# Map 1's shift in the differential attention: one reduce over adjacent columns instead of a minimum of two operands

## The chip, the cores and the metric

The kernel runs on one core of a Trainium2 chip. The metric is the time of one execution on the device in microseconds (us), less is better. The core's engines run side by side, each through its own list of instructions in order, and wait for each other by semaphores: TensorE (PE) multiplies matrices into PSUM, VectorE (DVE), ScalarE (ACT) and GpSimd (POOL) work on tiles of 128 partitions, and DMA queues, most of them fed by SyncE (SP), move data between the on-chip SBUF and the main memory.

## What is computed

The reference is a block of two layers on 2048 latent tokens and 256 context tokens of width 1024. In each layer one projection feeds four mixers side by side; their outputs are gated, projected and added to the stream. The change is in the first mixer, differential attention, of four heads with two attention maps each:

```python
def attend(qs, ks, vs):
    s = jnp.einsum('mbhqd,mbhkd->mbhqk', qs, ks).astype(F32) * scale
    p = jax.nn.softmax(s, axis=-1)
    w = (p[0] - lam * p[1]).astype(vs.dtype)
    return jnp.einsum('bhqk,bhkv->bhqv', w, vs)
...
o = lax.map(lambda qq: attend(qq, keys, vals), qb)
```

The latent tokens' queries see all 2304 keys. In the first layer there are also queries of the context tokens, which see the 256 context keys alone. The other three mixers are a gated linear recurrence, a windowed attention and an mLSTM.

## The kernel before

Each layer runs in three stages: first projections, then the loop of the differential attention, then the windowed attention, the two recurrences and the output projection. The rest of the layer's projections (`other_blocks`) are not given a stage of their own: they are the **filler** of the attention loop. `pump` issues filler matmuls until a given amount of TensorE work has been handed out, and is called with `FSTEP` between the two score products of a map and with `FGAP` after each map.

The loop goes over units of one head and 128 queries: 72 in layer 0 (of which 8 are context units) and 64 in layer 1. A unit does its map 1 first, then its map 0. `diff_scores(u, m)` (L1036 on) forms the scores of map `m` in two pieces of 1024 and 1280 keys, each in a PSUM buffer `scr` of its own that exists once. Behind each piece a `tensor_reduce` on DVE (L1048) takes the minimum over the keys into a column of the small tile `sm` (128 x 16): columns 2 and 3 for map 1, columns 0 and 1 for map 0. (The exponential is taken with a scale of -1, so the minimum plays the part of the maximum.) Then the minimum of the two columns becomes `u["nm"]`, the shift of the exponential: column 5 for map 1 (L1054), column 4 for map 0 (L1056, with a constant `shf` added). `diff_exp` (L1058 on) has ACT take the exponentials of both pieces out of PSUM with this shift, into tiles `p`, and their sums. Only then may PE write the next map's scores into the two buffers.

`diff_mix(u1, j)` works on the unit before, one piece at a call: for piece 0 three small instructions on `sm` (L1073 to L1075), and then for each piece one big DVE instruction that forms the weights from the two `p` tiles (L1082, by the helper `stt`, L111), a copy to 16 bits on ACT (L1084), the remainder as a subtraction on POOL (L1085, by the helper `tt`, L108), and a transposing DMA into `wt` (L1087). `tc.issue_after(u["nm"].ins)` puts the DVE instructions of `diff_mix` behind the new unit's `nm`. `diff_out` multiplies `wt` with the values of the unit before that one.

PE's order is the program's (`manual_schedule` for PE). The order of DVE, ACT, POOL and SP is made by a planner from planned durations, within the dependencies. In the profile, instructions of the helpers carry the helper's line: the minimum of L1054 stands as `L108 DVE TENSOR_TENSOR sm<-sm`, and the big DVE instruction as `L111 ... p<-p,sm,p`.

Of the kernel before, what the change touches and what calls it, by code (L numbers as in the profile page):

```python
# [15 lines left out]
ALU = mybir.AluOpType  # L16
# [13 lines left out]
AX = mybir.AxisListType  # L30
# [43 lines left out]
def kernel(  # L74
# [8 lines left out]
    V, A, G, PE, SP = nc.vector, nc.scalar, nc.gpsimd, nc.tensor, nc.sync  # L83
# [9 lines left out]
    def mm(o, lhsT, rhs, start, stop):  # L93
        PE.matmul(o, lhsT=lhsT, rhs=rhs, start=start, stop=stop)  # L94
        n = 1
        for d_ in rhs.shape[1:]:
            n *= d_
        pe_ns[0] += max(128, n * 4 if rhs.dtype == F32 else n) / 2.4
# [8 lines left out]
    def tt(e, o, a, b, op):  # L107
        return e.tensor_tensor(out=o, in0=a, in1=b, op=op)  # L108
# [150 lines left out]
    for l in range(n_layers):  # L259
# [768 lines left out]
        with ExitStack() as st2:  # L1028
# [4 lines left out]
            def halves_of(u):  # L1033
                return [(2048, 256)] if u["ctx"] else HALF

            def diff_scores(u, m):  # L1036


                sm, hs = u["sm"], halves_of(u)
                pss = u["s", m] = []  # L1040
                for j, (k0, n) in enumerate(hs):
                    ps = sps.tile([P, 1536 if j else 1024], F32, tag=f"sc{j}", name="scr")
                    for o in range(0, n, 512):
                        w = min(512, n - o)
                        mm(ps[:, o:o + w], u["Qs"][:, m, u["qo"]:u["qo"] + P], u["Ks"][m][:, k0 + o:k0 + o + w], True, True)
                    if j < len(hs) - 1:
                        pump(FSTEP * u["work"])
                    V.tensor_reduce(sm[:, m * 2 + j:m * 2 + j + 1], ps[:, :n], AX.X, ALU.min)  # L1048
                    pss.append(ps)
                o = m * 2  # L1050
                o2 = o + len(hs) - 1

                if m:
                    u["nm"] = tt(V, sm[:, 5:6], sm[:, o:o + 1], sm[:, o2:o2 + 1], ALU.min)  # L1054
                else:
                    u["nm"] = V.tensor_scalar(sm[:, 4:5], sm[:, o:o + 1], sm[:, o2:o2 + 1], shf, ALU.min, ALU.add)  # L1056

# [99 lines left out]
            def pump(ns):  # L1157
                owed[0] += ns
                while owed[0] > 0:
                    t0 = pe_ns[0]  # L1160
                    if next(filler, pump) is pump:
                        owed[0] = 0.0
                        break
                    owed[0] -= pe_ns[0] - t0
# [4 lines left out]
            with tc.manual_schedule(engines=MANUAL):  # L1169
                while True:  # L1170
                    u = next(it, None)
                    if u is None and u1 is None and u2 is None and u3 is None:
                        break
                    if u:
                        diff_scores(u, 1)
                    if u3:
                        diff_out(u3, 1)
                    pump(FGAP * (u["work"] if u else 1.0))
                    if u1:
                        with tc.issue_after(u["nm"].ins) if u else ExitStack():  # L1180
                            diff_mix(u1, 0)
                    if u:
                        diff_exp(u, 1)
                    if u3:
                        diff_norm(u3, 0)
                    if u:
                        diff_scores(u, 0)
                    if u3:
                        diff_norm(u3, 1)
                    if u2:  # L1190
                        diff_out(u2, 0)
                    pump(FGAP * (u["work"] if u else 1.0))
                    if u1:
                        with tc.issue_after(u["nm"].ins) if u else ExitStack():
                            diff_mix(u1, 1)
                    if u:
                        diff_exp(u, 0)
                    u1, u2, u3 = u, u1, u2
# [535 lines left out]
```

## Time and profile before

| | |
|---|---|
| median of 3 runs | 4100.06 us (4084.22 to 4102.09) |
| the profiled execution | 4102.18 us, span 4100.4 us |
| differential attention, layer 0 | 238 to 1260 us |
| differential attention, layer 1 | 2330 to 3285 us |
| busy over the span | PE 3358.2, DVE 2831.4, POOL 2375.0, ACT 2330.9 us |

Times in the trace are counted from the first instruction. A row of a timeline gives the start, the duration, engine, line, operation, the tile written and the tiles read (`out<-in`), the shapes, the count of instructions that are merged in the row, and in brackets the idle time of the engine before it with what ended it.

### The profile page before, as it was taken

Reading aid. Unit: us, or ns where it says so; the run is one execution under the profiler, and the core shown is the slowest. Engines: PE = TensorE matmul, PEld = TensorE weight load, DVE = VectorE, ACT = ScalarE, POOL = GpSimd, SP = SyncE. Lnnn points to the kernel's source line nnn. Section 1 sums busy time; section 2 is a strip of 40 time slices with the busy share of each in tenths; the row PEclk is TensorE's granted clock in tenths of the full one; section 3 lists DMA queues with packets and bytes.
Section 4 is the critical chain, followed back from the end, with each engine's and each line's share of the span. In section 5 each row is a group of like instructions: output and inputs, shape, how many; then the busy total and the mean of one; then the engine's idle time right before and its main releaser. Section 6 shows DMA issues by size and latency. Waiting matters only on the chain. (4 is left out here: it accounts for less than half of the span.)

```text
span 4100.4 us, 77666 instructions
## 1 busy us (share of the span) xinstructions
PE 3358.2 (82%) x29798; PEld 2269.8 (55%) x29798; DVE 2831.4 (69%) x4343; ACT 2330.9 (57%) x4662; POOL 2375.0 (58%) x1701
## 2 busy tenths in 40 slices
PE   6988878888768996888888988778887698758888
PEld 4656645444546765555557466444445476545554
DVE  5158888888896647465544398988888865467665
ACT  4245655556655636566654266656666665456764
POOL 4443455443445538798966535665334564488885
PEclk8999989999989995898889999999998899869999
DMA  6356866667656628577845457667676584366783
GB/s 211 91 149 150 186 136 159 140 141 154 145 128 157 161 95 200 149 194 185 205 119 177 126 125 151 135 140 155 148 162 142 125 193 116 106 162 170 183 194 104
DMA packets 1267259, 622.12 MB, mean 152 GB/s; under 512 B 931972, under 2 KB 1214152, under 8 KB 1266888
## 3 DMA queue, kind: packets, MB, share of 16 engines
q1 hardware_dynamic: 1164520, 490.65, 53.1%
q10 hardware_dynamic: 102368, 126.52, 9.2%
q8 instruction: 234, 3.83, 0.4%
q14 instruction: 137, 1.12, 0.1%
HBM read 291.76 MB, written 131.23 MB: 103 GB/s over the span
## 5 line engine op out<-in xcount | busy, mean ns | idle before, releaser
L108 POOL TENSOR_TENSOR p<-p,p 128x1024 f16<-128x1024 f32 (+2 forms) x264 | 629.4, 2385 | 792.7 <-ACT p L1084 722.8
L105 ACT ACTIVATE p<-scr,sm 128x1024 f32<-128x1024 f32 (+2 forms) x528 | 628.3, 1194 | 417.8 <-DVE sm L1073 145.2
L94 PE MATMUL ptm<-wb,hh 128*128 128x256 f16 (+2 forms) x5024 | 835.6, 273 | 32.6 <-DVE dSs L111 7.9
L1048 DVE TENSOR_REDUCE sm<-scr 128x1 f32<-128x1024 f32 (+2 forms) x528 | 699.3, 1327 | 218.3 <-PE scr L94 214.5
L94 PE MATMUL pfm<-hh,wb 128*128 128x512 f16 (+1 forms) x2592 | 805.7, 375 | 32.7 <-DVE gz L111 10.1
L94 PE MATMUL ptm<-wb,hl 128*128 128x256 f16 (+2 forms) x2512 | 672.1, 273 | 1.7 <-POOL hl L108 1.7
L94 PEld LDWEIGHTS <-wb 128*128 128x128 f16 x3888 | 378.1, 101 | 414.3 <-issue 84.0
L94 PE MATMUL scr<-Ks,Qs 128*128 128x512 f16 (+1 forms) x1296 | 364.8, 381 | 284.5 <-ACT p L105 279.4
L94 PEld LDWEIGHTS <-hh 128*128 128x128 f16 x5024 | 480.1, 100 | 133.9 <-issue 40.0
L94 PE MATMUL pfm<-hl,wb 128*128 128x512 f16 (+1 forms) x1296 | 485.6, 375 | 0.0
L111 DVE SCALAR_TENSOR_TENSOR p<-p,sm,p 128x1024 f32<-128x1024 f32 (+2 forms) x264 | 413.8, 1568 | 8.1
L94 PEld LDWEIGHTS <-Qs 128*128 128x128 f16 x1296 | 130.7, 102 | 425.2 <-issue 354.5
L94 PE MATMUL fx<-wo,mh 128*128 128x512 f16 x1088 | 342.4, 396 | 16.8 <-DVE xt L111 8.5
L1084 ACT CAST p<-p 128x1024 f16<-128x1024 f32 (+2 forms) x264 | 297.7, 1128 | 39.2 <-DVE p L111 33.8
L94 PEld LDWEIGHTS <-wt 128*128 128x128 f16 x4640 | 243.9, 102 | 71.4 <-DMA wt<-p 24.4
L94 PE MATMUL pv<-Vs,wt 128*128 128x128 f16 (+1 forms) x4640 | 258.5, 213 | 21.9 <-DMA wt<-p 13.5
L94 PEld LDWEIGHTS <-hl 128*128 128x128 f16 x2512 | 250.8, 100 | 35.4 <-POOL hl L108 3.4
L108 POOL TENSOR_TENSOR ph<-swp,ph 128x640 f16<-128x640 f32 (+2 forms) x136 | 196.0, 1442 | 53.7 <-ACT ph L1335 44.3
L108 POOL TENSOR_TENSOR E<-lk,cm 128x512 f32<-128x512 f32 (+1 forms) x136 | 204.8, 1506 | 34.6 <-DMA cm<-dhc 17.8
L94 PE MATMUL fx<-wo,mlo 128*128 128x512 f16 x544 | 212.9, 391 | 1.4 <-DVE mlo L108 1.1
L105 ACT ACTIVATE E<-E 128x1024 f32<-128x1024 f32 x136 | 143.2, 1054 | 102.8 <-POOL E L108 98.9
L108 DVE TENSOR_TENSOR QQ<-hq,E 128x512 f32<-128x512 f32 x119 | 143.8, 1214 | 65.2 <-ACT E L105 46.7
(301 smaller groups left out, 6577.2 us busy)
## 6 DMA issues: line engine op xcount, KB each, us to landing
wraw<-in_w_in_dram SPq DMA_DIRECT2D x60, 512.0 KB
dgt<-ga ACTq DMA_DIRECT2D x68, 256.0 KB
r1b<-dr SPq DMA_DIRECT2D x68, 256.0 KB
gtt<-dgt SPq DMA_DIRECT2D x34, 512.0 KB
mraw<-in_w_mod_dram SPq DMA_DIRECT2D x64, 256.0 KB
vi<-dhi SPq DMA_DIRECT2D x49, 256.0 KB
KSb<-dsk SPq DMA_DIRECT2D x56, 192.0 KB
Ks<-dka SPq DMA_DIRECT2D x64, 144.0 KB
```

The costliest lines, as they stand in the source:

```text
L94: PE.matmul(o, lhsT=lhsT, rhs=rhs, start=start, stop=stop)
L105: A.activation(out=o, in_=i, func=f, **kw)
L108: return e.tensor_tensor(out=o, in0=a, in1=b, op=op)
L111: V.scalar_tensor_tensor(out=o, in0=a, scalar=s, in1=b, op0=op0, op1=op1)
L1048: V.tensor_reduce(sm[:, m * 2 + j:m * 2 + j + 1], ps[:, :n], AX.X, ALU.min)
L1084: A.copy(wl[:, :n], p[:, :n])
```

## The change

The shift of map 1 is no longer the minimum of two operands of one column each, but a reduction over the columns `o` to `o2`, which lie side by side (one column in a context unit, where `o2 = o`). What is read, what is written and the value are the same. Map 0's line stays.

```diff
                 if m:
-                    u["nm"] = tt(V, sm[:, 5:6], sm[:, o:o + 1], sm[:, o2:o2 + 1], ALU.min)
+                    u["nm"] = V.tensor_reduce(sm[:, 5:6], sm[:, o:o2 + 1], AX.X, ALU.min)
                 else:
                     u["nm"] = V.tensor_scalar(sm[:, 4:5], sm[:, o:o + 1], sm[:, o2:o2 + 1], shf, ALU.min, ALU.add)
```

## Rows read from the trace of the kernel before

**Rows 1.** Busy time by stage: length; PE, PEld, DVE, ACT, POOL (instructions); clock, DMA, GB/s.
```profile
238.00:1260.00 1022.00, 819.92 (x7172) 541.44 (x7171) 856.91 (x1255) 602.00 (x990) 460.67 (x264) 0.93 0.66 149
...
2330.00:3285.00 955.00, 755.04 (x6579) 493.42 (x6578) 834.45 (x1162) 591.78 (x922) 468.85 (x257) 0.94 0.66 142
```

**Rows 2.** Groups by form, DVE: count, busy us, mean ns, idle before.
```profile
L111 DVE SCALAR_TENSOR_TENSOR p<-p,sm,p 128x1024 f32<-128x1024 f32 x128 | 172.3, 1346 | 7.6
...
L108 DVE TENSOR_TENSOR sm<-sm 128x1 f32<-128x1 f32 x136 | 97.8, 719 | 0.6
```

**Rows 3.** Instructions on tile sm, DVE: duration min/median/max in ns, first and last start.
```profile
L108 DVE TENSOR_TENSOR sm<-sm x136: 127/772/2330, 247.9 to 3240.4; 128x1 f32<-128x1 f32 x136
L1056 DVE TENSOR_SCALAR sm<-sm,shf x136: 244/272/277, 257.2 to 3248.0; 128x1 f32<-128x1 f32 x136
L1073 DVE TENSOR_REDUCE sm<-sm x136: 136/144/158, 263.0 to 3252.4; 128x2 f32<-128x4 f32 x128, 128x2 f32<-128x2 f32 x8
```

**Rows 4.** Timeline of DVE in one unit of layer 1.
```profile
2406.62 1.03 DVE L108 TENSOR_TENSOR sm<-sm 128x1 f32<-128x1 f32 x1
...
2408.33 1.28 DVE L111 SCALAR_TENSOR_TENSOR p<-p,sm,p 128x1024 f32<-128x1024 f32 x1
2409.63 1.22 DVE L1048 TENSOR_REDUCE sm<-scr 128x1 f32<-128x1024 f32 x1
2411.15 1.49 DVE L1048 TENSOR_REDUCE sm<-scr 128x1 f32<-128x1280 f32 x1 [0.30 <-PE scr L94]
2412.56 0.68 DVE L111 SCALAR_TENSOR_TENSOR tm<-ptm,bg 128x512 f32<-128x512 f32 x1
2413.16 0.27 DVE L1056 TENSOR_SCALAR sm<-sm,shf 128x1 f32<-128x1 f32 x1
```

**Rows 5.** Timeline of POOL in the same unit.
```profile
2405.02 2.61 POOL L108 TENSOR_TENSOR p<-p,p 128x1280 f16<-128x1280 f32 x1 [3.70 <-ACT p L1084]
2411.27 2.13 POOL L108 TENSOR_TENSOR p<-p,p 128x1024 f16<-128x1024 f32 x1 [3.63 <-ACT p L1084]
```

**Rows 6.** Timeline of ACT and PE in the same unit.
```profile
2407.74 1.11 ACT L105 ACTIVATE p<-scr,sm 128x1024 f32<-128x1024 f32 x1 [1.56 <-DVE sm L1073]
...
2407.85 0.27 PE L94 MATMUL ptm<-wb,hl 128*128 128x256 f16 x1
2409.00 0.59 PE L94 MATMUL scr<-Ks,Qs 128*128 128x512 f16 x2 [0.87 <-ACT p L105]
```

**Rows 7.** Timelines: first and last long minimum, a short one, POOL and PE beside.
```profile
246.96 2.12 POOL L108 TENSOR_TENSOR sn<-rp,sn 128x512 f32<-128x512 f32 x1
247.89 1.21 DVE L108 TENSOR_TENSOR sm<-sm 128x1 f32<-128x1 f32 x1
250.39 0.80 PE L94 MATMUL scr<-Ks,Qs 128*128 128x512 f16 x2 [2.70 <-ACT p L105]
...
2358.51 0.16 DVE L108 TENSOR_TENSOR sm<-sm 128x1 f32<-128x1 f32 x1
...
3220.22 2.61 POOL L108 TENSOR_TENSOR p<-p,p 128x1280 f16<-128x1280 f32 x1 [1.90 <-ACT p L1084]
3221.08 1.76 DVE L108 TENSOR_TENSOR sm<-sm 128x1 f32<-128x1 f32 x1
3225.73 0.63 PE L94 MATMUL scr<-Ks,Qs 128*128 128x512 f16 x1
```

**Rows 8.** Timelines of POOL and DVE at 780 us, and the group of this reduce.
```profile
778.59 2.13 POOL L108 TENSOR_TENSOR p<-p,p 128x1024 f16<-128x1024 f32 x1 [2.64 <-ACT p L1084]
780.19 0.68 DVE L1126 TENSOR_REDUCE drs<-sq 128x8 f32<-128x512 f32 x1
...
L1126 DVE TENSOR_REDUCE drs<-sq 128x8 f32<-128x512 f32 x16 | 10.8, 677 | 3.7 <-POOL sq L108 3.7
```

**Rows 9.** Who waited for whom, layer 0's loop, then layer 1's: us, times, longest.
```profile
PE scr L94 <- ACT p L105: 124.3, 86, 7.1
...
PE scr L94 <- ACT p L105: 155.1, 111, 6.3
```

## The prediction

> **What bounds the kernel now.** I read the busy time by stage first, then the instructions that touch the small tile `sm`, then one unit of the loop in order of time on four engines. The profiled execution took 4102.18 us for a span of 4100.4 us, so 1.8 us lie around the span; the median of the three runs is 4100.06 us, 2.1 us less, with runs from 4084.22 to 4102.09 us. I sum against 4102.2 us.
>
> The edited line runs in the diff attention alone, which fills 238 to 1260 us (layer 0, 72 units of 128 queries) and 2330 to 3285 us (layer 1, 64 units). There VectorE (DVE) is busy 856.9 of 1022 us and 834.5 of 955 us, 84% and 87%, against 80% and 79% for TensorE, and ScalarE and GpSimd (POOL) well below [rows 1]. So in these two stages DVE comes nearest to being the bound, but no engine is full: what holds a unit is partly a chain, reduce on DVE, shift `nm` on DVE, exponential on ACT, scores on PE, reduce again.
>
> The instruction that goes is the `tensor_tensor` of two one-column operands. It runs 136 times and takes 719 ns on the mean, 97.8 us in all [rows 2]; its shortest is 127 ns and its longest 2330 ns, though its shape never changes [rows 3]. Its twin for map 0 (L1056, the same minimum, the second column given as a scalar operand) lies between 244 and 277 ns in all its 136 runs [rows 3]. One unit shows why. At 2406.62 us the minimum starts and lasts 1.03 us, to 2407.65 [rows 4]; the POOL subtraction on `p`, two operands in SBUF, started at 2405.02 and ends at 2407.63 [rows 5]. The minimum ends as the POOL instruction ends. In the next half of the same unit the POOL subtraction runs from 2411.27 to 2413.40 [rows 5], and L1056 starts at 2413.16 and takes its usual 0.27 us under it [rows 4]. So, as these rows have it, with two SBUF tensor operands DVE waits for a running POOL `tensor_tensor`, and with one it doesn't.
>
> This holds over the run. Of the 136 minima 50 take 127 to 176 ns (one of them stands at 2358.51) and 86 take longer; of these 86, the first at 247.89 and the last at 3221.08 us, every one ends within 0.03 us of the end of a POOL `tensor_tensor` [rows 7]: 2.12 us from 246.96 for the first, 2.61 us from 3220.22 for the last.
>
> **The change part by part.** *Removed:* 136 minima, 97.8 us of DVE. *Added:* 136 reduces over two adjacent columns (one in the 8 context units). Nearest row: L1073, a reduce of `sm` from four columns to two, 136 to 158 ns [rows 3]. A reduce that reads 512 columns of SBUF takes 0.68 us at 780.19 while a POOL subtraction runs from 778.59 and 677 ns on the mean of its group [rows 8]: no hold. I take 0.146 us, bounds 0.127 (shortest minimum) to 0.277 (longest L1056). At 0.146 the adds cost 136 x 0.146 = 19.9 us and 97.8 - 19.9 = 77.9 us of held time leave this place; at 0.277, 60.1 us. *Moved:* nothing. What waits for `nm` and what `nm` waits for stay the same, and no wait is added.
>
> The Trainium skill (SBUF — State Buffer, Who interferes with whom) says that a VectorE instruction with two SBUF inputs contends with a GpSimd instruction that reads SBUF, that the loser blocks for the whole instruction, and that `tensor_reduce` never contends on trn2. That reaches past the rows, which have no two-column reduce under a POOL instruction: by it all 77.9 us leave this line. Where rows speak, they agree [rows 4, 5, 8]. Against the change speaks the Trainium skill (VectorE: DVE Perf Modes, Rules for kernel authors), which calls `tensor_reduce` the slowest DVE operation on a hot path; by it the new `nm` would lie at the upper bound, and 50 x 60.1 / 77.9 = 39 us would be left of the 50 below, 4063 us. For so few columns row L1073 says otherwise [rows 3].
>
> How much of 77.9 us reaches the end? Not all, since the wait can be met by the next two-operand instruction, and PE may not be ready sooner. In that unit [rows 4 to 6] the new `nm` ends at 2406.77, 0.88 us earlier.
> - DVE path. From the end of the minimum to the start of the big `p` instruction (L1082, by the helper at L111) lie the three small instructions L1073 to L1075, 2407.65 to 2408.33 = 0.68 us [rows 4]. None has two SBUF tensors; they run beside POOL and end at 2407.45; `p` has two SBUF operands and waits until 2407.65. So 0.68 us is the most that DVE gains here, and 0.20 us of the wait passes on to `p`.
> - ACT and PE path. The first exponential moves from 2407.74 to 2406.86 [rows 6]. PE stood 0.87 us waiting for it and starts the map 0 scores at 2409.00 [rows 6]; its filler before that ends at 2407.85 + 0.27 = 2408.12, so it can start at 2408.13, 0.87 us earlier. The second reduce (2411.15, after 0.30 us of waiting for PE's second scores [rows 4]) can then start at 2411.15 - 0.87 = 2410.28 as far as PE goes, and DVE is through with the first reduce at 2409.63 - 0.68 + 1.22 = 2410.17: 0.87 us earlier. The 0.30 us in which DVE stood idle make up what the DVE path lacks.
>
> So a unit saves at most its PE wait there, and at most its held time; where DVE has no idle time it saves what the DVE path gives. Worked out for each of the 86 held units (the first: held 1.06 us, PE waits 2.70; the last: held 1.61 us, PE waits 0, nothing saved through PE) [rows 7]: the lesser of held time and PE wait sums to 23.2 us in layer 0 and 33.9 us in layer 1, 57.0 us; capped also by the time to the next DVE instruction with two SBUF operands, 16.2 + 26.0 = 42.2 us. The PE waits behind this are there: PE waited 124.3 us and 155.1 us for exponentials in the two stages [rows 9]. I take 50 us, the middle, since units like the one above have DVE idle time and reach the upper figure, while those crowded with filler work on DVE don't: 4102.2 - 50 = 4052 us. After each loop the next stage's PE work is queued behind it in PE's written order, so the end moves by the same amount; POOL, busy 45% and 49% of these stages [rows 1], has room for its part.
>
> **The rivals.**
> - *All of it comes through* (or more, if the order improves too): 77.9 us, 4024 us. For it: the chain through ACT and PE carries the whole held time where PE waits long enough. Against: PE waits less than the held time in many units (0.87 against 0.88 here, none in the last). Chance 0.08.
> - *The wait only changes its name.* PE has its filler matmuls and a fixed amount of them; once the scores come sooner it meets the next wait, the landing of the transposed weights or the map 1 scores of the next unit. The `p` instruction already meets POOL: its mean is 1.346 us against 1.28 us undisturbed [rows 2, 4]. If every unit kept only a fifth of 77.9 us, 15.6 us, the time is 4087 us; if nothing, or if the hold were that of reading the column just written, which a reduce would share, 4102 us. Against the latter stand the 50 minima of 127 to 176 ns, which read the column just written as well [rows 7]. Chance 0.16.
> - *Slower: the planned order moves.* PE's order is written out by hand, but that of DVE, ACT, POOL and the queues comes from planned durations. If `nm` is planned otherwise, a filler instruction may go ahead of it on DVE, as `tm` (0.68 us at 2412.56) goes ahead of L1056 [rows 4], and it then sits on the chain. At 0.68 us each the 50 us are gone from 50 / 0.68 = 74 units on, and with one in each of the 136 units it is 4052 + 92.5 = 4145 us; over 0.5% slower needs 104 units. For it: nothing fixes the place. Against: `nm` stays behind the same reduce, and both forms cost about the same when not held. Chance 0.08.
>
> **How the numbers follow.** The forecast, 25 to 75 us saved (4027 to 4077 us), has 0.68; the rivals 0.08, 0.16 and 0.08 as above. The range reaches past the full gain by a little over the half width of the three runs' spread (9 us), to 4015 us, and up to 4096 us, which takes in most of the second rival and none of the third: 0.8 in all. Measurement can tell 0.5% here, some 20.5 us, so faster means under 4079.6 against the median: the forecast, the full gain and a sliver of the second rival, 0.77; same 0.15; slower 0.08.
>
> **What would show it.** Right: the group of `sm<-sm` reduces at L1054 with a mean near 0.146 us and a maximum under 0.28; DVE busy time down by about 78 us less what `p` takes over; the mean of `p` 128x1024 up from 1.346 us by about (77.9 - 53)/128 = 0.2 us, where 53 us is the DVE path's sum over the 86 units before the cap by PE; PE's wait for exponentials down by some 50 us from 124.3 + 155.1 = 279.4 us [rows 9]; both stages shorter, layer 1 by more than layer 0, and the other stages as before. Wrong: reduces at L1054 that still end with POOL instructions (then it isn't the operands), PE waits that only change their releaser (second rival), or filler instructions between the last reduce and `nm` in units that had none (third).

## The result, and the profile after

The changed kernel takes 4037.63 us (median of 5 runs, 4030.76 to 4042.67) against 4095.77 us of the kernel before (5 runs): a ratio of 0.9852 with a 95% interval of 0.9828 to 0.9875, or 51 to 70 us less. Run again later (e10), it came out at 0.9841 (0.982 to 0.9862). The forecast was 4052 us, 50 us less.

First the instruction itself. Instructions on tile `sm` on DVE in the changed kernel (duration min/median/max in ns, first and last start), as in [rows 3]:

```profile
L1054 DVE TENSOR_REDUCE sm<-sm x136: 122/144/155, 249.0 to 3182.9; 128x1 f32<-128x2 f32 x128, 128x1 f32<-128x1 f32 x8
L1056 DVE TENSOR_SCALAR sm<-sm,shf x136: 241/272/275, 257.2 to 3190.6; 128x1 f32<-128x1 f32 x136
```

And the groups by form (count, busy us, mean ns, idle before), as in [rows 2]:

```profile
L111 DVE SCALAR_TENSOR_TENSOR p<-p,sm,p 128x1280 f32<-128x1280 f32 x128 | 235.7, 1841 | 0.0
L111 DVE SCALAR_TENSOR_TENSOR p<-p,sm,p 128x1024 f32<-128x1024 f32 x128 | 186.2, 1455 | 7.6
...
L1054 DVE TENSOR_REDUCE sm<-sm 128x1 f32<-128x2 f32 x128 | 18.4, 144 | 0.3
...
L1054 DVE TENSOR_REDUCE sm<-sm 128x1 f32<-128x1 f32 x8 | 1.2, 150 | 0.2
```

No shift of map 1 is held any more: 155 ns at most where it was 2330, though 84 of the 136 still start while a POOL `tensor_tensor` has more than 0.2 us to run. The 97.8 us of [rows 2] are 19.6 us. The big instruction on `p` now meets POOL more often: its first piece went from 1346 to 1455 ns on the mean.

The unit of [rows 4 to 6], in the changed kernel: the timelines of POOL, DVE, ACT and PE from one unit's map 1 shift on.

```profile
2383.46 2.62 POOL L108 TENSOR_TENSOR p<-p,p 128x1280 f16<-128x1280 f32 x1 [4.09 <-ACT p L1084]
...
2384.67 0.14 DVE L1054 TENSOR_REDUCE sm<-sm 128x1 f32<-128x2 f32 x1
...
2385.49 1.66 DVE L111 SCALAR_TENSOR_TENSOR p<-p,sm,p 128x1024 f32<-128x1024 f32 x1
2387.08 2.73 DVE L1048 TENSOR_REDUCE sm<-scr 128x1 f32<-128x1024 f32 x2
2389.73 0.68 DVE L111 SCALAR_TENSOR_TENSOR tm<-ptm,bg 128x512 f32<-128x512 f32 x1
2390.32 0.27 DVE L1056 TENSOR_SCALAR sm<-sm,shf 128x1 f32<-128x1 f32 x1
...
2384.91 1.11 ACT L105 ACTIVATE p<-scr,sm 128x1024 f32<-128x1024 f32 x1 [0.68 <-DVE sm L1073]
...
2386.17 0.59 PE L94 MATMUL scr<-Ks,Qs 128*128 128x512 f16 x2
```

The shift takes 0.14 us while POOL's subtraction runs on to 2386.08. `p` starts under that subtraction and takes 1.66 us, 0.38 us more than the 1.28 us of [rows 4]. PE doesn't wait for the exponential, and DVE has no idle time between its two reduces (merged in one row) where it had 0.30 us. From map 1's shift to map 0's it is 2390.32 - 2384.67 = 5.65 us; in [rows 4] it was 2413.16 - 2406.62 = 6.54 us. So 0.89 us are gone; the prediction's working for this unit gave 0.87.

Busy time of the two loops (from the first L1048 reduce of a layer to the end of the last; columns as in [rows 1]):

```profile
238.90:1228.00 989.10, 812.02 (x7108) 535.20 (x7107) 816.71 (x1241) 597.30 (x982) 461.69 (x260) 0.94 0.69 152
2311.70:3190.50 878.80, 716.25 (x6378) 474.10 (x6377) 773.61 (x1127) 574.12 (x890) 451.78 (x245) 0.95 0.70 149
```

In the kernel before the same two loops:

```profile
238.20:1248.70 1010.50, 811.73 (x7108) 535.92 (x7107) 845.70 (x1241) 597.24 (x982) 452.98 (x260) 0.94 0.67 149
2330.60:3248.00 917.40, 730.88 (x6379) 479.09 (x6378) 807.50 (x1126) 572.45 (x890) 446.76 (x245) 0.94 0.66 142
```

So by the two profiles loop 0 gives 21.4 us and loop 1 gives 38.6 us, 60.0 together; the start and the two stages outside the loops give 3.9 us of the spans' difference of 63.9 us. PE's idle time in the loops fell from 198.8 + 186.5 to 177.1 + 162.6 us, 45.6 us. The rest, 14.6 us in loop 1, is PE busy for a shorter time with the same matmuls, at a granted clock of 0.95 after 0.94, that is with less time at the lower one of its two levels (1.2 and 2.4 GHz). This part can't be put down to the change: loop 1 has 0.95 in e8 with the old minimum too, and 0.93 in e5 with the reduce.

Who waited for whom in the changed kernel's loops, as in [rows 9]:

```profile
PE scr L94 <- ACT p L105: 111.7, 71, 6.6
...
PE scr L94 <- ACT p L105: 133.1, 96, 6.5
```

One execution's loop is a coarse measure: loop 1 of one and the same plan lay between 878.8 and 882.9 us in two profiles. The table gives both loops for every kernel that ran, and PE's idle time in the two together (their length less PE's busy time); the first two rows (the minimum in both layers) have the same loops but for one fill, and so have the next four (the reduce in both layers).

| kernel | loop 0 | loop 1 | sum | PE idle | whole, ratio to before (95%) |
|---|---|---|---|---|---|
| before | 1010.5 | 917.4 | 1927.9 | 385.3 | |
| e8, before with one more fill | 1012.2 | 910.9 | 1923.1 | 383.4 | 1.0002 (0.9986 to 1.0018) |
| changed | 989.1 | 878.8 | 1867.9 | 339.6 | 0.9852 (0.9828 to 0.9875) |
| e10, changed again | 992.0 | 882.9 | 1874.9 | 338.5 | 0.9841 (0.982 to 0.9862) |
| e9, changed with one more fill | 992.3 | 880.0 | 1872.3 | 339.5 | 0.9847 (0.9828 to 0.9867) |
| e5, changed, more reduces outside the loops | 989.8 | 884.9 | 1874.7 | 337.5 | 0.99 (0.9868 to 0.9932) |
| e1, scalar operand in map 1 | 992.2 | 886.8 | 1879.0 | 344.5 | 0.9885 (0.9864 to 0.9906) |
| e2, two SBUF tensors in map 0 | 998.8 | 891.0 | 1889.8 | 347.2 | 0.9899 (0.9882 to 0.9915) |
| e3, old minimum behind the new shift | 1001.8 | 903.8 | 1905.6 | 363.4 | 0.9947 (0.9932 to 0.9961) |
| e4, before with POOL's subtraction as a fill | 940.6 | 868.3 | 1808.9 | 292.0 | 0.9689 (0.9673 to 0.9704) |
| e6, layer 0 alone | 996.3 | 910.5 | 1906.8 | 366.5 | 0.9882 (0.9844 to 0.992) |
| e6, layer 1 alone | 1012.1 | 888.6 | 1900.7 | 361.8 | 0.9941 (0.9926 to 0.9956) |
| e7, the three small ones earlier | 988.8 | 900.2 | 1889.0 | 360.9 | 0.9923 (0.9896 to 0.995) |
| e11, changed, a third `p` buffer | 987.6 | 877.5 | 1865.1 | 333.7 | 0.984 (0.9814 to 0.9865) |

The mean of the loops' sum is 1925.5 us over before and e8, and 1872.5 us over the changed kernel, e10, e9 and e5: 53 us less. PE's idle time is the steadier number: 384.3 us on the mean of the same two and 338.8 us of the same four, none over 1.3 us from its mean, so 45.5 us less. The other 7.5 us are PE's busy time for the same matmuls, which differs by as much between profiles of one form (1528.3 and 1537.3 us in the changed kernel and e5).

### The profile page after: what moved, and what is told of

Read it like the earlier page. It is cut to its first block, busy times and chain, and to the rows that moved or that the text cites. A ratio compares the mean times of both kernels' runs of the same rounds, so it can differ in the third digit from the quotient of the medians.

```text
span 4036.5 us, 77667 instructions
## 1 busy us (share of the span) xinstructions
PE 3352.6 (83%) x29798; PEld 2267.3 (56%) x29798; DVE 2780.1 (69%) x4343; ACT 2326.5 (58%) x4662; POOL 2386.3 (59%) x1701
## 5 line engine op out<-in xcount | busy, mean ns | idle before, releaser
L1048 DVE TENSOR_REDUCE sm<-scr 128x1 f32<-128x1024 f32 (+2 forms) x528 | 698.1, 1325 | 214.3 <-PE scr L94 211.2
L111 DVE SCALAR_TENSOR_TENSOR p<-p,sm,p 128x1024 f32<-128x1024 f32 (+2 forms) x264 | 429.3, 1627 | 8.1
L1084 ACT CAST p<-p 128x1024 f16<-128x1024 f32 (+2 forms) x264 | 297.3, 1126 | 45.6 <-DVE p L111 36.2
L94 PE MATMUL pv<-Vs,wt 128*128 128x128 f16 (+1 forms) x4640 | 255.0, 212 | 19.8 <-DMA wt<-p 12.7
```

Of the source, the lines that this page charges most:

```text
L111: V.scalar_tensor_tensor(out=o, in0=a, scalar=s, in1=b, op0=op0, op1=op1)
L1084: A.copy(wl[:, :n], p[:, :n])
```

## The experiments

The theory: a DVE instruction with two tensor operands in SBUF waits for a POOL instruction that reads SBUF, and the wait sat on the loop's chain. Its rivals: something of the reduce or of the planned order makes the gain; or the wait cost DVE's own queue alone, or only the exponentials behind it.

**e1, another form with one tensor operand.** Map 1's shift as map 0's: the second column is a scalar operand.

```diff
-u["nm"] = V.tensor_reduce(sm[:, 5:6], sm[:, o:o2 + 1], AX.X, ALU.min)
+u["nm"] = V.tensor_scalar(sm[:, 5:6], sm[:, o:o + 1], sm[:, o2:o2 + 1], None, ALU.min)
```

> Map 1's shift in a third form: one tensor column, the other as scalar operand, as in map 0's line; the value is the same. If the number of SBUF tensor operands decides, none of the 136 is held: mean near 0.27 us, maximum under 0.28 us, also where a POOL subtraction runs, and the time is that of the changed kernel plus at most 136 x (0.271 - 0.144) = 17 us: 4038 to 4055 us. If it is something of the reduce (its order in the plan, its own way of reading), the held 86 come back and the time is 4085 to 4100 us.

4052.44 us (4 runs) against 4099.21. Instructions on `sm` in this kernel:

```profile
L1054 DVE TENSOR_SCALAR sm<-sm x136: 183/204/215, 248.1 to 3196.4; 128x1 f32<-128x1 f32 x136
```

None is held: 215 ns at most, and 83 of them start with over 0.25 us of a POOL `tensor_tensor` to run. So it isn't the reduce that does it: for this one-column minimum it is the second SBUF tensor operand, and a scalar per partition doesn't count as one. It is no rule for every form with one SBUF tensor operand. In the kernel before these two have one as well:

```profile
L638 DVE COPY gates<-tm x36: 158/168/2122, 250.0 to 2516.2; 128x16 f32<-128x16 f32 x36
L366 DVE TENSOR_SCALAR bcol<-bcol x8: 155/156/2151, 43.9 to 2163.5; 128x2 f32<-128x2 f32 x8
```

Nine of the copies and two of the `tensor_scalar` instructions start with over 0.15 us of a POOL `tensor_tensor` to run, and all eleven last to its end, within 0.03 us. The loops are 6.5 us longer than the changed kernel's mean, for 136 x (204 - 144) ns = 8.2 us more on the chain. The mean, 204 ns, is under the 0.27 us expected, and the time lies in the range given for it.

**e2, the hold set up at map 0.** The changed kernel, with the constant `shf` as a second SBUF tensor.

```diff
-u["nm"] = V.tensor_scalar(sm[:, 4:5], sm[:, o:o + 1], sm[:, o2:o2 + 1], shf, ALU.min, ALU.add)
+u["nm"] = V.scalar_tensor_tensor(out=sm[:, 4:5], in0=sm[:, o:o + 1], scalar=sm[:, o2:o2 + 1], in1=shf, op0=ALU.min, op1=ALU.add)
```

> The changed kernel with map 0's shift given a second SBUF tensor operand (the constant shf as tensor, the second column as scalar); the value is the same. In the trace of the changed kernel POOL subtractions still run for 41 us in all beyond the end of the 136 map 0 shifts (91 of them start under one). Two operands: some 90 of them are now held, to the end of a POOL instruction, and their sum rises from 36.5 to about 78 us. Then: if a held shift costs through ACT and PE (the exponentials come later), the time rises by 25 to 41 us, to 4063 to 4079 us. If it costs through DVE's own queue alone, nothing is lost, since the big two-operand instruction on p follows the shift within 0.2 us and waits for the same POOL instruction anyway: 4038 us within 8.

4056.63 us (4 runs) against 4099.21. Instructions on `sm` in this kernel, and then the group of `p` by form:

```profile
L1056 DVE SCALAR_TENSOR_TENSOR sm<-sm,shf x136: 188/368/1806, 258.1 to 3209.3; 128x1 f32<-128x1 f32 x136
```

```profile
L111 DVE SCALAR_TENSOR_TENSOR p<-p,sm,p 128x1280 f32<-128x1280 f32 x128 | 213.6, 1669 | 0.0
```

The hold came, as it should: the longest went from 275 to 1806 ns, and the sum from 36.5 to 67.6 us, 31 us more (fewer were held than expected, 72, all of them to the end of a POOL instruction). The `p` behind it waited less by 235.7 - 213.6 = 22 us, so DVE as a whole was busy only 8.5 us longer (2788.6 after 2780.1). Still the loops are 17 us longer than the changed kernel's mean, 8 of them idle time of PE, and the whole's ratio is 0.9899 where the changed kernel had 0.9852 and 0.9841, some 20 us. That is less than the 25 to 41 us expected of the exponentials' chain and more than the none expected of DVE's queue. At most 8.5 us of it can be DVE's own longer queue; what is left says that a held shift costs through the exponentials even where the next DVE instruction would have waited for the same POOL instruction.

**e3, the hold without a reader.** The changed kernel with the old minimum behind the new shift, into a column that nobody reads; the instructions that stood behind the shift stand behind it.

```diff
 u["nm"] = V.tensor_reduce(sm[:, 5:6], sm[:, o:o2 + 1], AX.X, ALU.min)
+with tc.issue_after(u["nm"].ins):
+    u["nm"] = tt(V, sm[:, 15:16], sm[:, o:o + 1], sm[:, o2:o2 + 1], ALU.min)
```

> The changed kernel with the old two-operand minimum put in again right behind the new shift, into a column that nobody reads: DVE's queue meets the old hold at the old place, but the exponentials don't wait for it. About 80 us of hold come back on DVE. If the gain of the change came through ACT and PE alone, the time stays at 4038 to 4046 us; if it came through DVE's own queue alone, it goes back to 4090 to 4100 us. By the sums of the prediction (42 us through DVE at least, 57 through ACT and PE at most) it should lie between, near 4075 us, since the next scores' first reduce waits behind the held instruction, the three small ones and p.

4076.98 us (4 runs) against 4099.21. Instructions on `sm`:

```profile
L1054 DVE TENSOR_REDUCE sm<-sm x136: 123/145/156, 247.3 to 3221.4; 128x1 f32<-128x2 f32 x128, 128x1 f32<-128x1 f32 x8
L108 DVE TENSOR_TENSOR sm<-sm x136: 139/725/2268, 247.3 to 3221.4; 128x1 f32<-128x1 f32 x136
```

The whole hold is back on DVE, at the old length, and the shift is free of it. The loops lie between: 1905.6 us, 33 us over the changed kernel's mean and 20 under the mean of before and e8, and PE's idle time lies between as well (363.4 us). The time is the expected one (near 4075 us). So neither path alone carries the gain. The shares are less sure than these two numbers: the reduce stands here beside the minimum, 136 x 0.145 = 19.7 us more on DVE than in the kernel before, and whatever of it reached the end belongs to neither path. That leaves 13 to 33 us for DVE's own queue and 20 to 40 us for the exponentials.

**e4, POOL writes only.** The kernel before, with the remainder's subtraction replaced by a fill of the same bytes.

```diff
-tt(G, wl[:, n:2 * n], p[:, :n], wl[:, :n], ALU.subtract)
+G.memset(wl[:, n:2 * n], 0.0)
```

> The kernel before (two-operand minimum), with the POOL subtraction of the weights' remainder replaced by a POOL fill of the same bytes: the remainder is left out of the output. POOL then writes SBUF there but reads nothing. If the hold is between two readers of SBUF, 75 of the 86 held minima (those that ended with this subtraction) fall to about 0.15 us and some ten stay held by POOL's filler instructions, and the big instruction on p loses its holds too (means 1.28 and 1.54 us). If it were any POOL instruction that is running, they are still held, to the end of the fill.

3971.22 us (4 runs) against 4099.21. Instructions on `sm`, and then the fill's group by form:

```profile
L108 DVE TENSOR_TENSOR sm<-sm x136: 131/150/1224, 247.0 to 3124.7; 128x1 f32<-128x1 f32 x136
```

```profile
L1085 POOL MEMSET p<- 128x1280 f16 x128 | 149.3, 1166 | 402.7 <-DVE p L111 304.1 <-ACT p L105 53.5 <-issue 25.7
```

The two-operand minimum is quick once the subtraction is gone: 27.1 us in all instead of 97.8. Twelve are still held (199 to 1224 ns), each to the end of a POOL `tensor_tensor` of the filler. By the minima alone this doesn't tell reading from writing: the fill doesn't wait for ACT's copy, so it starts earlier, is half as long, and only 3 of the minima start under one (none of these is held). What they show is that the subtraction is the cause of the held time. Other instructions of the same trace do tell it. With the 3 minima, 20 DVE instructions with two SBUF tensor operands (4 on `p`, 8 of `rp` with `cs`, 5 of `rp` with `sn`) start with 0.1 us or more of a fill to run, and each takes the time that it takes alone, as this one under 1.06 us of a fill:

```profile
674.81 1.16 POOL L1085 MEMSET p<- 128x1280 f16 x1
674.91 0.69 DVE L108 TENSOR_TENSOR rp<-rp,cs 128x512 f32<-128x512 f32 x1 [1.17 <-POOL sn L108]
```

Of six more on `bch`, five aren't held either; the sixth stands behind a held copy and ends with it. The one `rp` with `cs` of this shape that starts under a POOL `tensor_tensor` here takes 1.52 us. So a POOL instruction that only writes SBUF doesn't hold these, while it does hold the copy `gates<-tm` of e1's lines: three that start under a fill last 628 to 916 ns, to its end. The big instruction on `p` didn't lose its holds as expected: its means are 1.34 and 1.60 us, since 13 of each 128 still meet a `tensor_tensor` of the filler. The 128 us are those of a computation with its remainder left out, and of transposes that start earlier.

**e6, one layer at a time.** The reduce in layer 0 or in layer 1 alone (`if l == 0:` or `if l == 1:` around the new line, the old one else).

> The reduce in layer 0 alone; layer 1 keeps the minimum of two operands. If each loop's gain is its own, loop 0 is 20 us shorter than before (238 to 1248.7 us before, 21.4 us less with the whole change) and loop 1 as before within 5 us: a total of some 20 us under the kernel before, 4076 us. If a part of the whole change's gain comes from the planned order in the stages outside the loops (those summed to -4 us in the profiled runs), the total differs from that by some us either way.

> The reduce in layer 1 alone. If each loop's gain is its own, loop 1 is 35 to 39 us shorter (917.4 us before, 878.8 with the whole change) and loop 0 as before: some 37 us under the kernel before, 4060 us. By the prediction's cap (a unit saves at most PE's wait before its next scores) it would be 34 us or less in loop 1; more than that shows that the cap was too tight.

Layer 0 alone: 4051.09 us (4 runs), layer 1 alone 4071.44 us (10 runs), against 4093.35: 42 and 22 us less. The totals came the other way round than expected. The loops didn't: loop 0 alone is 15 us under the mean of before and e8 with loop 1 at its value of e8, and loop 1 alone is 26 us under with loop 0 unchanged. PE's idle time says the same: with layer 0 alone 182.6 us in loop 0 (198.8 before) and 183.9 in loop 1 (186.5 before), with layer 1 alone 199.0 and 162.7. In the profile of layer 0 alone the stage between the loops took 1071.3 us (before: 1081.9) and the last one 838.7 (852.4), which nothing edited explains. In e8, with the minimum in both layers, the stage between the loops took 1071.3 us as well.

**e8 to e10, a new plan with nothing in it.** One fill of a column that nobody reads, in one unit of layer 0, in the kernel before (e8) and in the changed one (e9), and the changed kernel again (e10).

```diff
+if m and u["start"] and u["h"] == 0 and l == 0:
+    V.memset(sm[:, 15:16], 0.0)
```

> The kernel before with one fill of one column of sm, which nobody reads, in the first unit of layer 0: 0.06 us of DVE work, but the plan of everything behind it is made anew. What the total and the stages outside the loops move by is what a new planned order is worth by itself. If the order does little: the kernel before within 5 us. If the 10 to 14 us by which the stages outside the loops differed between the profiles (layer 0 alone against before) come from the order, it moves by as much, either way. The loops must stay within 5 us of before.

> The same fill in the changed kernel. Against the kernel with the same fill and the two-operand minimum, this is the change once more under another plan: the loops together shorter by 50 to 60 us, the total by 45 to 65 us, whatever the two fills do to the stages outside.

> The changed kernel as it is, on the chip and beside the runs of these two. The first result was a ratio of 0.9852 (0.9828 to 0.9875). Loops: 989.1 and 878.8 us in its first profile; the kernel with more reduces outside, whose loops are the same, had 989.8 and 884.9 us. If the second loop's 38.6 us of gain (more than the sum of the prediction allowed) is the usual value, it comes again within 3 us; if one execution's chance, it lies nearer to 33 us.

e8: 4096.44 us (12 runs), e9: 4035.05 (5 runs), e10: 4030.13 (5 runs), against 4095.28 (17 runs). A new plan by itself is worth nothing that can be measured (1.0002), and the change is worth the same with it (e9 against e8: 61 us) as without (65 us). One profile's stage, though, is off by 10 us with no cause in the edit (e8's 1071.3 us), and its loop 1 by 6.5 us. In both PE was busy for a shorter time with the same matmuls: 915.4 us after 930.0 in the stage, at a granted clock of 0.90 after 0.88, and 723.4 us after 730.9 in the loop, at 0.95 after 0.94. So the stage times of a single profile don't settle differences of that size, and for e6 it stays open why layer 0 alone gave 42 us. The second loop's 38.6 us of gain came down to 34.5 and 37.4 us in e10 and e9 and 32.5 in e5.

**e5, the same edit elsewhere.** The changed kernel with two more minima and sums of this kind as reduces, in the stages outside the loops.

```diff
-tt(V, dn, dn, TM[:, 2, d, js[d] * 4:js[d] * 4 + 4], ALU.max)
+V.tensor_reduce(dn, dn2[:, 0:2].rearrange("p r h -> p h r"), AX.X, ALU.max)
...
-tt(V, sm[:, 3], sm[:, 3], sm[:, 2], ALU.add)
-V.reciprocal(sm[:, 4], sm[:, 3])
+V.tensor_reduce(sm[:, 4], sm[:, 2:4].rearrange("p r h -> p h r"), AX.X, ALU.add)
+V.reciprocal(sm[:, 4], sm[:, 4])
```

> The changed kernel with the same edit at two more places outside the loops: the sum of two groups of four columns in the windowed attention (34 times) and the maximum of two groups of four in the mLSTM (68 times) as reduces over a pair, for which ACT copies the second group beside the first (68 small copies). Same values. Held time there, from the kernel before: 68 x (0.630 - 0.150) + 34 x (0.584 - 0.150) = 47 us of DVE. If it counted as in the loops, 25 us or more less: 4013 us or under. But DVE is busy only 53% and 64% of these stages and nothing shows it on their path: I expect 0 to 12 us less, and the planned order moves by as much.

4056.74 us (4 runs) against 4093.35. The two groups, which took 41.2 and 18.9 us in the changed kernel:

```profile
L1428 DVE TENSOR_REDUCE dn<-dn 128x4 f32<-128x8 f32 x68 | 10.6, 156 | 52.8 <-ACT dn L105 52.7
...
L1358 DVE TENSOR_REDUCE ssm<-ssm 128x4 f32<-128x8 f32 x34 | 5.3, 155 | 12.9 <-ACT ssm L105 12.4 <-ACT swp L105 0.4
```

44 us of held time are gone from DVE, and nothing of it reached the end: the last stage took 854.9 us, after 845.9 and 845.2 in the changed kernel's two profiles, and the whole was some 20 us slower than the changed kernel (0.99 after 0.9852), where 0 to 12 us less were expected. There DVE waits for ACT anyway: 52.7 us ahead of the `dn` reduce, after 41.5 ahead of the old maximum. The 68 added copies run on ACT as well, so what the reduces would give without them isn't told apart.

**e7, the three small instructions earlier.** L1073 to L1075 of the unit before, moved behind the first reduce of map 1's scores.

```diff
 V.tensor_reduce(sm[:, m * 2 + j:m * 2 + j + 1], ps[:, :n], AX.X, ALU.min)
 pss.append(ps)
+if v and j == 0 and len(hs) == 2:
+    three(v)
```

> The changed kernel with the three small instructions of the unit before (sums, reciprocal, factor) moved from behind map 1's shift to behind the first reduce of map 1's scores, where DVE often waits for PE (0.3 to 0.6 us). With the change p is let go by POOL at the old place in the held units, so that nothing is won there; in the 50 units without a hold p starts 0.68 us sooner, up to 34 us. Against it: the three take longer (0.6 us) than many of those idle times, and then push map 1's second reduce, and the shift, back. By the first 4010 to 4030 us, by the second 4038 to 4060 us.

4065.22 us (5 runs) against 4093.35: the second outcome. Loop 0 is as in the changed kernel, loop 1 18 us longer than its mean (900.2 against 881.7). PE's idle time grew there, 181.0 us after 162.6. That the three instructions push the shift back is the expected reason; it isn't shown.

**e11, a third buffer.** In the changed kernel ACT's exponentials wait for the transposing DMA, which reads the `p` buffer that they are to overwrite. ACT's idle time ahead of its instructions on `p`, changed kernel:

```profile
  DVE sm L1056: 139.8, 69
  DVE sm L1073: 84.5, 74
...
  DMA wt<-p: 12.7, 18
```

In the kernel before it was 3.5 us in 6 places. e11 gives map 0's second piece one more buffer and pays for it with tiles cut to size.

```diff
-p = da.tile([P, 1280], F32, tag=f"p{m}", name=f"p{m}", bufs=4)
+p = da.tile([P, 1280 if j else 1024], F32, tag=f"p{m}{j}", name=f"p{m}", bufs=2 if m or not j else 3)
...
-wt = da.tile([P, 20, P], F16, tag="wt", name="wt")
+wt = da.tile([P, 20 if j else 16, P], F16, tag=f"wt{j}", name="wt", bufs=1)
```

> The changed kernel with a third buffer for map 0's second p tile (the one that the transposing DMA reads), paid for by cutting the first pieces' p and wt tiles to the size they need; the other tiles alternate as before. In the changed kernel ACT's exponentials wait 12.7 us in 18 places for that DMA, in the kernel before 3.5 us in 6: if that is the wait that took a part of the gain back, it falls to about 0 and the loops get shorter by 5 to 12 us together, 4022 to 4034 us in all. If the second halves of the units are held by something else (DVE's reduces, PE's filler), the wait goes and the loops stay within 4 us.

4027.77 us (5 runs) against 4094.39. The wait is gone; these are the three longest that are left:

```profile
  DVE sm L1056: 140.2, 70
  DVE sm L1073: 76.8, 73
  DVE p L111: 46.3, 29
```

and the loops sum to 1865.1 us, 7 us under the changed kernel's mean. Its ratio of 0.984 beats the kernel before; from the changed kernel's (0.9841 and 0.9852) it can't be told apart.

## Why the prediction was right, point by point

- *The hold and its cause*: right. 0.146 us a reduce was forecast, 0.144 measured; 77.9 us of held time were to leave this line, 97.8 - 19.6 = 78.2 us did. e1 and e2 show that for the one-column shift the second SBUF tensor operand decides, and e4 that POOL's subtraction is what is waited for, and that a POOL fill held none of 20 instructions with two SBUF tensor operands. The prediction's "with one it doesn't" holds for the rows it names and not in general: the copies and `tensor_scalar` instructions shown at e1 have one and are held. (The longest of the 50 short minima is 174 ns in the trace, not 176.) The Trainium skill (SBUF — State Buffer, Who interferes with whom) has `tensor_reduce` free of this contention on trn2. The 155 ns at most agree. The Trainium skill (VectorE: DVE Perf Modes, Rules for kernel authors) calls `tensor_reduce` on a hot path the slowest DVE operation. For two columns the measurement differs: 144 ns, against 150 for the unheld minimum of e4.
- *How much reaches the end*: the working gave 42.2 to 57.0 us and I took 50; the loops gave 53 us, the whole 58 (51 to 70). The two ends can be weighed against the trace by cutting each unit at map 0's shift (changed kernel's profile against that before, 86 held units). In the 39 units where PE's wait was at least as long as the hold (to within 0.05 us), 28.7 us were held, and the first half of these units got 28.4 us shorter, the second halves none. In the 47 units where PE's wait was shorter, 49.0 us were held and the lesser of the two sums to 28.4 us; their first halves got 37.1 us shorter and their second halves 9.1 us longer, 28.0 us net. That is 56.4 us in all, near the cap by PE's wait, 57.0 us; but PE was also busy 14.3 us less in this profile, which isn't that cap's doing. In e10, with PE busy 6.2 us less than before, it is 31.6 - 8.0 + 36.9 - 8.4 = 52.1 us. Profiles with about the same busy time of PE differ by 48 us (e10 against e8) and 51 us (e9's loop 0 and e5's loop 1 against before). So the loops came out between the two caps, where the forecast was. The other cap, 42.2 us, by the next two-operand instruction on DVE, was passed by 3 us (PE's idle time) to 11 us (the loops' mean), which fits that DVE's idle time made up for a part of it; it isn't shown unit by unit. That the middle of the two was the right place was a judgement and no sum, and so in part luck. Of the 8 us by which the forecast was under the result, 3 are in the loops' mean; the other 5 don't show in single profiles of the stages outside, and where they come from stays open.
- *Which path*: I had the two paths side by side; e3 shows both at work (13 to 33 us through DVE's own queue, 20 to 40 through the exponentials), and e2 that the second one is there where DVE's own queue gets at most 8.5 us longer.
- *By layer*: layer 1 more than layer 0, as forecast: 32.5 us against 26.0 to 33.9, and 20.6 us against 16.2 to 23.2 (means of the four and the two).
- *The wait that changes its name* (second rival): a small part. `p` took over 13.9 us on its first pieces, 0.11 us each where I had 0.2; ACT's wait for the transposing DMA rose from 3.5 to 12.7 us. Whether it is a part of what the second halves gave back isn't shown: e11 takes it away, and there the second halves of the held units are still 11.4 us longer than before. What holds them stays open.
- *The planned order* (third rival): no filler moved in front of the shift in a way that cost: other DVE instructions stand between the last reduce and the shift in 118 units before and 121 after, for 104 and 103 us in all; e8 shows that a new plan by itself moves the total by nothing measurable.
- *What would show it*: DVE's busy time fell by 2831.4 - 2780.1 = 51.3 us, where I had named 78 us less `p`'s share. That share came to 15.6 us over all pieces (25 us by the prediction's 0.2 us each); the remaining 11 us are the net of many small changes, the largest rises in other instructions with two SBUF operands (`QQ` 6.8, `rp` with `cs` 5.1 us). PE's wait for exponentials fell by 34.6 us to 244.8, not by 50, as the rest of PE's shorter time is spread over other waits and, in loop 1, the clock.

## What to carry to other kernels

Compare one shape's shortest and longest duration. Where a tiny DVE instruction sometimes takes many times its minimum, see whether its long runs end with POOL's instructions, as all 86 did here. Another form can take that wait away: here a reduce over adjacent columns, or a scalar operand, for two operands of one column. Check the new form's own longest duration too, since copies and `tensor_scalar` instructions of two columns and more are held here with a single SBUF tensor operand. It pays where that instruction stands on the chain between engines; where its engine waits for others anyway, 44 us less of it brought nothing (e5, with the copies that it needed). To size it, take for each place the lesser of the hold and the wait of the engine that comes last; that gave 57 us here, an upper end, against 53 in the loops.

## What the runs showed of the hardware that I had not expected

A `scalar_tensor_tensor` on one column with two SBUF tensors and a scalar operand takes 188 ns when it isn't held, less than the 241 ns at least of the `tensor_scalar` with two scalar operands that it replaced (e2). And a hold on one column of 128 values can last 2.3 us, nearly the whole of POOL's 2.6 us, though the instruction itself needs 0.13 us. A POOL fill and a POOL `tensor_tensor` hold different things: both hold the copy `gates<-tm`, and only the second was seen to hold an instruction with two SBUF tensor operands (e1, e4).
